# A two-layer decoder step: residual of the retention's output projection turned by VectorE's 32x32 transposes, with tiles of every second column

## The chip, the cores and the metric

The kernel runs on one core of a Trainium2 chip. The metric is the device time of one execution in microseconds (us); the time before is the median of three runs. The engines are TensorE (PE, with its weight loads as PEld), VectorE (DVE), ScalarE (ACT), GpSimd (POOL) and SyncE (SP). DMAs are issued by SP and by ACT; each of these issues in program order and waits in that order.

## The reference

One inference step of a trunk with two layers, for a prompt of 1024 tokens and for 8 single decode tokens (rows of x_sample). Layer one is multi-scale retention, layer two sliding-window attention; both are pre-normalized and residual. What matters here is the seam between them:

```python
    o = rmsnorm(o, g_out.reshape(RET_HEADS, RET_DV)).reshape(B, L, RET_V)
    o = o * jax.nn.silu(gate)
    return x + o @ w_out, S.astype(S0.dtype)
...
    h = rmsnorm(x, g_norm)
    proj = h @ w_in
```

D_MODEL is 1024, RET_V is 2048. So x + o @ w_out is a sum over 2048 features for 1024 output features and 1032 tokens, and its result, times a gain per feature, is the input of the attention's projection (w_in_swa, 1024 x 2304). All is float32.

## The kernel before

**Number format.** Every float32 operand of a large product is split into a high part (`hi`) and the rest (`lo`); a product is three matmuls (hi by hi, hi by lo, lo by hi) into one PSUM tile. The high part of a weight is made by ACT, the low part by DVE or POOL.

**Stages.** First the retention's input projection and the decode tokens' state update (up to about 540 us of the span), then the retention over chunks (`steps`, 32 of them, to about 690), then the output projection (`ro_` functions, about 683 to 878), then the attention layer (to the end). In the first two stages and in the block that holds `ro_ahead(2)` all engines run in program order; in the others PE does, and a planner orders ACT, DVE, POOL and SP.

**The output projection.** Activations are kept transposed (features on partitions, tokens along the row), so a result tile is 128 output features (`ft`, 8 of them) by a group of tokens (`gi`; `RG` is 0 to 512, 512 to 768, 768 to 1032). `ro_part` (L1197) adds 8 of the 16 blocks of 128 features in, three matmuls each; a tile has two parts (`kh`). The tiles of `gi` 0 come first, `ft` 0 to 7, then `gi` 1 and 2 for each `ft`. The weights come in slots of 1024 x 256 (`wslot`, L1137): two raws of 512 KB by SP, each converted in four pieces of 128x256, L1147 on ACT and L1148 on DVE, with the gain of the retention's output norm. Raws have two buffers (`wr`), slots three. `ro_ahead` (L1189) starts slots ahead of their use.

**The residual.** `ro_xr` (L1222) loads the x rows of a tile by SP (tile `xr`, two buffers; for `gi` 2 also 8 decode rows), and `ro_finish` (L1231) turns each 128x128 block on PE, through `tr` (L101), straight into the tile's PSUM sum:

```python
            for i in range(nfull):
                tr(ps[:, i * 128:i * 128 + 128], xr[:, i, :], ident, start=False, stop=(i == nfull - 1))
```

Then ACT copies the sum into `x1` (L1250), and for each 256 tokens ACT and DVE make the parts of the attention's input, `A_hi` and `A_lo`, from PSUM with the gain `gk` (L1252, L1253); ACT squares and POOL adds up for the norm; ACT stores `x1` to the scratch `xscr` (L1260). PSUM tiles come from two pools of 2 and 4. `reload2` (L1262) brings the first 512 tokens back from `xscr`, since `A_hi` holds the retention's output until then; the last projection of the attention layer (`so_all`, L1788) reads `xscr` once more as its residual.

**The early tile.** Tile (0, 0) is computed within the last two steps of the retention, in `b_wmm` (L1047). Its weights are loaded by `b_w` (L1026) in four loads of 512 rows by 128 columns and converted by `b_wc` (L1032) into `woh` and `wol`, its x rows by `b_x` (L1043). They stand in rings of tiles (`ring`, L163; `EV` at L161 gives the buffers: p 3, x 2, c 2, w 2), which the steps use for q and k (p), v (x) and the gate (c, w). A load into a ring waits until the tile that had the buffer is read: a q tile by b_ql on POOL (L812), a v tile by b_vl (L800). The loop over the steps is at L1078; `others` (L1059) is the order of a step's work on ACT, DVE and POOL; b_sq (L983, a square on ACT), b_ts (L991, DVE), b_pw (POOL, L116) and b_on (L999, DVE) normalize a chunk, and b_tr turns it on PE. A head's last state is stored by ACT's queue (L973, tile `sf`).

**Gains.** `small_loads` and `gains` turn three gain vectors into columns (`gcol`), early in the first stage.

Of the kernel before, what the change touches and what calls it, by code (L numbers as in the profile page):

```python
# [7 lines left out]
F32 = mybir.dt.float32  # L8
# [62 lines left out]
def _trunk(ctx, tc, nc, a):  # L71
# [17 lines left out]
    xscr = dp.tile([8, 128, NT], F32, name="xscr")  # L89
# [316 lines left out]
    gl = sp.tile([25, 128], F32, name="gl")  # L406
    rT = sp.tile([128, 7, 4, 4], F32, name="rT")
# [225 lines left out]
    later(15, lambda: act(gcol, heads[0].pop("pg")[:, :25], AF.Copy))  # L633
# [392 lines left out]
    def b_w(i):  # L1026

        t = ring("px"[i // 2])[:, 0:512].rearrange("p (k f) -> p k f", k=4)
        nc.sync.dma_start(out=t, in_=w_out_ret[i * 512:i * 512 + 512, 0:128].rearrange("(k p) f -> p k f", p=128))
        wo[i] = t  # L1030

    def b_wc(i):  # L1032

        raw = wo[i]
        hi, lo = [(woh[i + 2 * (x == "l")] if i < 2 else rp.tile([128, DV], F32R, tag="v" + x, name="wo" + x, bufs=2))
                  .rearrange("p (k f) -> p k f", k=4) for x in "hl"]
        for k in range(4):
            gk = gcol[:, 4 * i + k:4 * i + k + 1]
            act(hi[:, k], raw[:, k], AF.Copy, scale=gk)
            dve.scalar_tensor_tensor(lo[:, k], raw[:, k], gk, hi.bitcast(F32)[:, k], MUL, SUB)  # L1040
        wo[i] = hi, lo

    def b_x():  # L1043
        wo["x"] = ring("c")[:, 0:512].rearrange("p (c f) -> p c f", c=4)
        nc.sync.dma_start(out=wo["x"], in_=x_prompt[0, 0:512, 0:128].rearrange("(c p) f -> p c f", p=128))

    def b_wmm(i):  # L1047
# [3 lines left out]
        hi, lo = wo[i]  # L1051
# [26 lines left out]
    for i in range(-1, NS + 2):  # L1078
# [23 lines left out]
        for n in {NS - 2: (0,), NS - 1: (1, 2), NS: (3,)}.get(i, ()):  # L1102
            b_wc(n)
# [127 lines left out]
    def ro_finish(ft, gi):  # L1231
# [4 lines left out]
        if ft + gi:  # L1236
            if (ft, gi) not in ro_x:
                ro_xr(ft, gi)
# [765 lines left out]
```

## Time and profile before

| | us |
|---|---|
| three runs | 1313.51, 1311.6, 1314.25 |
| median | 1313.51 |
| profiled execution, its own time | 1314.25 |
| its span | 1312.2 |
| PE busy | 1284.0 (98%) |
| PEld busy | 1212.2 (92%) |
| DVE busy | 727.7 (55%) |
| ACT busy | 691.4 (53%) |
| POOL busy | 630.8 (48%) |

The profile is one execution on the chip. Matmuls overlap in their pipeline, so the busy time of a group of them is no measure of what one costs; the distance between the starts of neighbours is. "Idle before" stands in brackets, with what ended it. A line of a timeline joins neighbours of one kind (x4); its duration is that of all of them.

### The profile page before, as it was taken

The page shows a single profiled execution, that of the slowest core. Times are in us where ns is not written, and L with a number is a line of the kernel's source. Part 1 is how long each engine was busy: PE and PEld are TensorE (multiplying, and loading weights), DVE is VectorE, ACT ScalarE, POOL GpSimd, SP SyncE. Part 2 cuts the span into 40 slices and gives each one's busy share as a digit, 9 for nine tenths or more (in the row PEclk, how much of TensorE's full clock was granted, in tenths as well). Part 3 has the DMA queues.
Part 4 walks back from the last instruction along what each step waited for, and adds up shares of the span by engine and source line. Part 5 has one row for each costly group of instructions (what it writes and reads, how often), then busy time and mean ns, then how long its engine had stood idle before and what let it go on. Part 6 is the DMA issues. An engine that isn't in the chain of part 4 may idle for free.

```text
span 1312.2 us, 26102 instructions
## 1 busy us (share of the span) xinstructions
PE 1284.0 (98%) x9597; PEld 1212.2 (92%) x9597; DVE 727.7 (55%) x1476; ACT 691.4 (53%) x1722; POOL 630.8 (48%) x800
## 2 busy tenths in 40 slices
PE   6999999999999999999999999999999999999998
PEld 6999999999999999887887889999999999998998
DVE  6944556565565564477785333324665666766321
ACT  5533544554555653577775444445576666666121
POOL 6654544545445544599980110137476676554000
PEclk9999999999999999999999999999998999999999
DMA  6314767677676854456556554353032211237232
GB/s 225 104 61 129 238 197 244 180 234 220 197 239 184 247 174 138 132 169 213 177 165 193 162 165 123 122 147 85 17 106 72 65 58 44 75 110 251 73 96 78
DMA packets 199907, 193.98 MB, mean 148 GB/s; under 512 B 12916, under 2 KB 180140, under 8 KB 199764
## 3 DMA queue, kind: packets, MB, share of 16 engines
q1 hardware_dynamic: 165024, 157.78, 39.2%
q10 hardware_dynamic: 34756, 34.53, 8.3%
q8 instruction: 76, 1.25, 0.4%
q14 instruction: 51, 0.42, 0.1%
HBM read 132.23 MB, written 61.08 MB: 147 GB/s over the span
## 4 chain that ended last, share of the span: by engine, by line
PE 91%; DVE 2%; ACT 2%; DMA 2%; POOL 2%; issue 1%; ACTq 0%; SPq 0%; POOLq 0%; DVEq 0%
PE b L331 7%; PE b L332 7%; PE b L333 7%; PE pj L1167 6%; PE pj L1168 6%; PE pj L1169 6%; PE tr L101 4%; PE b L324 4%; PE b L325 4%; PE b L326 4%; PE pj L1214 4%; PE pj L1215 4%; PE pj L1216 4%; PE o L1645 2%; PE b L538 2%; PE sc L1610 1%
## 5 line engine op out<-in xcount | busy, mean ns | idle before, releaser
L331 PE MATMUL b<-xh,woh 128*128 128x258 f32 x784 | 223.2, 285 | 0.0
L333 PE MATMUL b<-xh,wol 128*128 128x258 f32 x784 | 221.7, 283 | 0.0
L332 PE MATMUL b<-xl,woh 128*128 128x258 f32 x784 | 221.6, 283 | 0.0
L1167 PE MATMUL pj<-A_hi,wh 128*128 128x384 f32 (+1 forms) x512 | 174.9, 342 | 1.7 <-ACT A_hi L1670 1.3
L1168 PE MATMUL pj<-A_lo,wh 128*128 128x384 f32 (+1 forms) x512 | 165.2, 323 | 0.1
L1169 PE MATMUL pj<-A_hi,wl 128*128 128x384 f32 (+1 forms) x512 | 165.1, 322 | 0.0
L331 PEld LDWEIGHTS b<-xh,woh 128*128 128x128 f32 x784 | 148.0, 189 | 4.1 <-issue 3.7
L332 PEld LDWEIGHTS b<-xl,woh 128*128 128x128 f32 x784 | 148.7, 190 | 0.0
L333 PEld LDWEIGHTS b<-xh,wol 128*128 128x128 f32 x784 | 148.0, 189 | 0.0
L222 POOL TENSOR_TENSOR wol<-raw,woh 128x512 fp32r<-128x512 f32 x52 | 68.1, 1318 | 130.9 <-ACT woh L217 128.8
L324 PE MATMUL b<-woh,xh 128*128 128x256 f32 x448 | 126.6, 283 | 0.0
L325 PE MATMUL b<-wol,xh 128*128 128x256 f32 x448 | 126.0, 281 | 0.0
L326 PE MATMUL b<-woh,xl 128*128 128x256 f32 x448 | 125.6, 280 | 0.0
L1167 PEld LDWEIGHTS pj<-A_hi,wh 128*128 128x128 f32 x512 | 97.3, 190 | 5.4 <-issue 2.6
L1168 PEld LDWEIGHTS pj<-A_lo,wh 128*128 128x128 f32 x512 | 97.5, 190 | 0.4 <-DVE A_lo L1671 0.4
L1169 PEld LDWEIGHTS pj<-A_hi,wl 128*128 128x128 f32 x512 | 96.9, 189 | 0.0
L1148 DVE SCALAR_TENSOR_TENSOR wl<-wr,gcol,wh 128x256 fp32r<-128x256 f32 x128 | 53.8, 486 | 68.2 <-ACT wh L1147 68.2
L1259 POOL TENSOR_TENSOR acc<-acc,sq 128x256 f32<-128x256 f32 (+1 forms) x28 | 20.6, 742 | 146.4 <-ACT sq L1258 146.3
L1625 POOL TENSOR_TENSOR s<-s,sm 128x512 f32<-128x512 f32 x64 | 66.5, 1039 | 47.7 <-DVE sm L1624 43.5
L324 PEld LDWEIGHTS b<-woh,xh 128*128 128x128 f32 x448 | 84.3, 188 | 5.0 <-issue 2.9
L326 PEld LDWEIGHTS b<-woh,xl 128*128 128x128 f32 x448 | 84.3, 188 | 0.0
L325 PEld LDWEIGHTS b<-wol,xh 128*128 128x128 f32 x448 | 84.3, 188 | 0.0
(391 smaller groups left out, 3636.6 us busy)
## 6 DMA issues: line engine op xcount, KB each, us to landing
raw<-in_w_in_ret_dram ACTq DMA_DIRECT2D x44, 512.0 KB
st<-in_state_ret_dram SPq DMA_DIRECT2D x64, 256.0 KB
out_dram<-st SPq DMA_DIRECT2D x64, 256.0 KB
wr<-in_w_out_ret_dram SPq DMA_DIRECT2D x32, 512.0 KB
wr<-in_w_in_swa_dram SPq DMA_DIRECT2D x18, 512.0 KB
vb<-vscr SPq DMA_DIRECT2D x64, 128.0 KB
evp<-qks SPq DMA_DIRECT2D x32, 256.0 KB
evx<-vsc SPq DMA_DIRECT2D x32, 256.0 KB
```

The lines of the kernel that those rows point to most:

```text
L222: eng.tensor_tensor(lo, src_of(s, name, sub), hi.bitcast(F32), SUB)
L324: mm(dst, xh, wh, start=a and i == 0, stop=False, skip_group_check=True)
L325: mm(dst, xh, wl, start=False, stop=False, skip_group_check=True)
L326: mm(dst, xl, wh, start=False, stop=z, skip_group_check=True)
L331: mm(dst, wh, xh, start=a, stop=False, **sg)
L332: mm(dst, wh, xl, start=False, stop=False, **sg)
L333: mm(dst, wl, xh, start=False, stop=z, **sg)
L1148: nc.vector.scalar_tensor_tensor(lo[:, k, :], raw[:, k % 4, :], gk, hi.bitcast(F32)[:, k, :], ALU.mult, ALU.subtract)
L1167: mm(ps, hi[:, k, fs], xh[:, k, t0:t1], start=first and k == ks[0], stop=False)
L1168: mm(ps, hi[:, k, fs], xl[:, k, t0:t1], start=False, stop=False)
L1169: mm(ps, lo[:, k, fs], xh[:, k, t0:t1], start=False, stop=last and k == ks[-1])
L1625: nc.gpsimd.tensor_tensor(st[:, :, 0:256], st[:, :, 0:256], sm.unsqueeze(2).broadcast_to([128, 2, 256]), ALU.mult)
```

## The change

A result tile no longer holds 128 neighbouring features but every second one of 256: feature 256 pr + 2 q + u stands at partition q of tile ft = 2 pr + u. So ACT and DVE read the weights of w_out_ret with a step of two columns, the gains of the attention's norm get columns in that order, and the rows of w_in_swa are loaded as pairs of rows per partition, in two transfers per raw (`rows_load`). The x rows are loaded for 256 tokens and 256 features at once, in four transfers of 32 partitions each, so that blocks of 32x32 already stand where they belong but for the turn within a block; DVE turns the blocks (`nc.vector.transpose`) and adds the PSUM sum. The scratch gets the shape [4, 128, 2, tokens]. The early tile's weights come in eight loads of 256 rows by 256 columns, of which half the columns are used; its residual (two loads) is still turned by PE.

```diff
-    xscr = dp.tile([8, 128, NT], F32, name="xscr")
+    xscr = dp.tile([4, 128, 2, NT], F32, name="xscr")
...
+        for u in range(2):
+            tr(pg[:, 32 + 4 * u:36 + 4 * u], gs.rearrange("a (p u) -> a u p", u=2)[:, u], ident[:4, :4])
...
+                        (gs, norm_swa.rearrange("o (a f) -> (o a) f", a=4)),
...
+        act(gcol[:, 16:24].rearrange("p (a u) -> p u a", u=2), pg[:, 32:40].rearrange("p (u a) -> p u a", u=2), AF.Copy)
...
+    def b_w(i, tag):
+
+        wo[i] = ring(tag)[:, 0:512].rearrange("p (k f) -> p k f", k=2)
+        nc.sync.dma_start(out=wo[i], in_=w_out_ret[i * 256:i * 256 + 256, 0:256].rearrange("(k p) f -> p k f", p=128))
+
+    def b_x(i, tag):
+
+        t = ring(tag)[:, 0:512].rearrange("p (c f) -> p c f", c=2)
+        nc.sync.dma_start(out=t, in_=x_prompt[0, 256 * i:256 * i + 256, 0:256].rearrange("(c p) f -> p c f", p=128))
+        wo["x", i] = t.rearrange("p c (q u) -> p c u q", u=2)[:, :, 0]
...
+        raw = wo[i].rearrange("p k (q u) -> p k u q", u=2)[:, :, 0]
...
+        for k in range(2):
+            gk = gcol[:, 2 * i + k:2 * i + k + 1]
+            act(hi[:, 2 * b + k], raw[:, k], AF.Copy, scale=gk)
+            dve.scalar_tensor_tensor(lo[:, 2 * b + k], raw[:, k], gk, hi.bitcast(F32)[:, 2 * b + k], MUL, SUB)
...
-        if i in (NS - 3, NS - 2):
-            b_w(i - NS + 3)
-        if i in (NS - 2, NS - 1):
-            b_w(i - NS + 4)
-        if i == NS - 1:
-            b_x()
+        for n, tag in {NS - 3: ((0, "p"),), NS - 2: ((1, "p"), (4, "x"), (2, "p")),
+                       NS - 1: ((5, "x"), (6, "c"), (3, "p"), (7, "p"))}.get(i, ()):
+            b_w(n, tag)
+        if i == NS:
+            b_x(0, "x")
+            b_x(1, "w")
...
-        for n in {NS - 2: (0,), NS - 1: (1, 2), NS: (3,)}.get(i, ()):
+        for n in {NS - 2: (0, 1), NS - 1: (2, 4, 3, 5), NS: (6, 7)}.get(i, ()):
...
+    def rows_load(raw, src, j):
+        for a in (0, 1):
+            r0 = 512 * j + 256 * a
+            nc.sync.dma_start(out=raw[:, 2 * a:2 * a + 2], in_=src[r0:r0 + 256].rearrange("(p u) f -> p u f", u=2))
...
+                h2, l2 = [t[:, k, :].rearrange("p (u q) -> p u q", u=2) for t in (hi, lo)]
+                r2 = raw[:, k % 4, :].rearrange("p (q u) -> p u q", u=2)
...
+                nc.scalar.activation(h2, r2, AF.Copy, scale=gk)
+                nc.vector.scalar_tensor_tensor(l2, r2, gk, h2.bitcast(F32), ALU.mult, ALU.subtract)
...
+    def ro_xd():
+        nc.gpsimd.memset(xd, 0.0)
+        v = x_sample[:, 0, :].rearrange("i (a b f) -> b i a f", a=4, b=4)
+        for b in range(4):
+            nc.sync.dma_start(out=xd[32 * b:32 * b + 8], in_=v[b])
+        for u in range(2):
+            nc.vector.transpose(xdT[:, :, u, :], xd.rearrange("p a (j u) -> p u a j", u=2)[:, u])
+
+    def ro_xr(pr, a):
+
+        xr = ro_x[pr, a] = fp.tile([128, 8, 64], F32, name="xr", bufs=4)
+        v = x_prompt[0, a:a + 256, 256 * pr:256 * pr + 256].rearrange("(a i) (b f) -> b i a f", i=32, b=4)
+        for b in range(4):
+            nc.sync.dma_start(out=xr[32 * b:32 * b + 32], in_=v[b])
...
-            if gi == 2:
-                tr(ps[:, 256:264], xr[0:8, 2, :], ident[:8, :8], start=False, stop=False)
-            for i in range(nfull):
-                tr(ps[:, i * 128:i * 128 + 128], xr[:, i, :], ident, start=False, stop=(i == nfull - 1))
...
-            pv = ps[:, a - t0:b - t0]
-            x1 = fp.tile([128, 264], F32, name="x1", bufs=2)
-            nc.scalar.activation(x1[:, :n], pv, AF.Copy)
+            x1 = fp.tile([128, 264], F32, name="x1", bufs=3)
+            if ft + gi == 0:
+                nc.vector.tensor_copy(x1[:, 0:256], ps[:, a - t0:a - t0 + 256])
+            else:
+                if (pr, a) not in ro_x:
+                    ro_xr(pr, a)
+                xr = ro_x[pr, a].rearrange("p a (j u) -> p u a j", u=2)
+                nc.vector.transpose(x1[:, 0:256], xr[:, u])
+                nc.vector.tensor_tensor(x1[:, 0:256], ps[:, a - t0:a - t0 + 256], x1[:, 0:256], ALU.add)
+            if n > 256:
+                nc.vector.tensor_tensor(x1[:, 256:264], ps[:, 256:264], xdT[:, pr, u, 0:8], ALU.add)
             if gi > 0:
-                nc.scalar.activation(A_hi[:, ft, a:b], pv, AF.Copy, scale=gk)
-                nc.vector.scalar_tensor_tensor(A_lo[:, ft, a:b], pv, gk, A_hif[:, ft, a:b], ALU.mult, ALU.subtract)
+                nc.scalar.activation(A_hi[:, ft, a:b], x1[:, :n], AF.Copy, scale=gk)
+                nc.vector.scalar_tensor_tensor(A_lo[:, ft, a:b], x1[:, :n], gk, A_hif[:, ft, a:b], ALU.mult, ALU.subtract)
...
-            nc.scalar.dma_start(out=xscr[ft, :, a:b], in_=x1[:, :n])
+            nc.scalar.dma_start(out=xscr[pr, :, u, a:b], in_=x1[:, :n])
...
         ro_finish(0, 0)
-        for ft in (1, 2):
-            ro_xr(ft, 0)
+        for a_ in (0, 256):
+            ro_xr(0, a_)
+        ro_xd()
```

## Rows read from the trace of the kernel before

**Rows 1.** The page's busy table, PE, and its chain by engine
```profile
PE 1284.0 (98%) x9597; PEld 1212.2 (92%) x9597; DVE 727.7 (55%) x1476; ACT 691.4 (53%) x1722; POOL 630.8 (48%) x800
...
PE 91%; DVE 2%; ACT 2%; DMA 2%; POOL 2%; issue 1%; ACTq 0%; SPq 0%; POOLq 0%; DVEq 0%
```

**Rows 2.** Instructions of L101 that read xr: count, ns min/median/max, first and last
```profile
L101 PE MATMUL pj<-ident,xr x68: 224/272/328, 707.6 to 877.8; 128*128 128x128 f32 x60, 8*128 8x8 f32 x8
```

**Rows 3.** Stretches: length, then busy us of PE, PEld, DVE, ACT, POOL, clock, DMA share, GB/s
```profile
705.00:710.00 5.00, 5.00 (x26) 4.07 (x25) 2.90 (x8) 3.87 (x10) 0.00 (x0) 1.00 0.86 257
...
820.00:840.00 20.00, 20.00 (x169) 19.84 (x168) 9.11 (x22) 10.92 (x27) 3.23 (x4) 1.00 0.43 129
```

**Rows 4.** Timeline of PE around three groups of transposes: start, duration, instruction
```profile
720.27 0.40 PE L1215 MATMUL pj<-A_lo,wh 128*128 128x512 f32 x1
720.50 0.39 PE L1216 MATMUL pj<-A_hi,wl 128*128 128x512 f32 x1
...
721.40 0.40 PE L1215 MATMUL pj<-A_lo,wh 128*128 128x512 f32 x1
...
784.71 0.28 PE L1216 MATMUL pj<-B_hi,wl 128*128 128x256 f32 x1
...
785.18 0.28 PE L1215 MATMUL pj<-B_lo,wh 128*128 128x264 f32 x1
...
790.73 0.28 PE L1216 MATMUL pj<-B_hi,wl 128*128 128x264 f32 x1
...
791.49 0.28 PE L1215 MATMUL pj<-B_lo,wh 128*128 128x256 f32 x1
```

**Rows 5.** Timeline of PE, its two waits after 710 us
```profile
714.66 0.51 PE L1216 MATMUL pj<-A_hi,wl 128*128 128x512 f32 x1 [0.23 <-DVE wl L1148]
...
717.78 0.51 PE L1214 MATMUL pj<-A_hi,wh 128*128 128x512 f32 x1 [0.52 <-ACT wh L1147]
```

**Rows 6.** Timeline of DVE: a cast in SBUF and an operation on PSUM, 128x256 each
```profile
671.43 0.28 DVE L806 CAST qh<-evp 128x256 fp32r<-128x256 f32 x1
...
672.82 0.48 DVE L775 SCALAR_TENSOR_TENSOR kl<-tr,M,kh 128x256 fp32r<-128x256 f32 x1
```

**Rows 7.** Timeline of SP's DMA issues, 675 to 710 us
```profile
675.78 0.38 SPq L1029 DMA_DIRECT2D evp<-in_w_out_ret_dram  x1
...
688.67 11.15 SPq L1144 DMA_DIRECT2D wr<-in_w_out_ret_dram  x4
699.98 0.94 SPq L1226 DMA_DIRECT2D xr<-in_x_prompt_dram  x2
703.64 6.25 SPq L1144 DMA_DIRECT2D wr<-in_w_out_ret_dram  x3
```

**Rows 8.** Timeline of POOL, the last read of a q tile
```profile
679.67 0.79 POOL L812 TENSOR_TENSOR ql<-evp,qh 128x256 fp32r<-128x256 f32 x1
```

**Rows 9.** Timeline of ACT and its DMA issues, 681 to 709 us
```profile
681.78 1.26 ACT L1039 ACTIVATE woh<-evp,gcol 128x128 fp32r<-128x128 f32 x4
...
684.12 0.57 ACT L987 ACTIVATE on<-po 128x512 f32<-128x512 f32 x1
...
685.78 0.38 ACTq L973 DMA_DIRECT2D out_dram<-sf  x1
...
695.59 3.31 ACT L1147 ACTIVATE wh<-wr,gcol 128x256 fp32r<-128x256 f32 x8 [4.61 <-PE S L101]
...
707.23 1.71 ACT L1147 ACTIVATE wh<-wr,gcol 128x256 fp32r<-128x256 f32 x4
```

**Rows 10.** Timeline of DVE, a chunk's scaling and the low parts of a raw
```profile
686.70 0.75 DVE L999 TENSOR_SCALAR on<-po,bss 128x512 f32<-128x512 f32 x1 [0.73 <-POOL bss L116]
...
710.75 1.69 DVE L1148 SCALAR_TENSOR_TENSOR wl<-wr,gcol,wh 128x256 fp32r<-128x256 f32 x4 [1.26 <-ACT wh L1147]
```

**Rows 11.** Timeline of PE, the last chunk's transposes
```profile
689.00 0.60 PE L101 MATMUL tr<-ident,on 128*128 128x128 f32 x4
```

**Rows 12.** Waits of SP's queue, 670 to 900 us: total, times, longest
```profile
SPq L1144 <- DMA out_dram<-sf: 9.7, 1, 9.7
```

More of the change, by code (lines that the diff above doesn't have):

```diff
@@ L406, in _trunk @@
     gl = sp.tile([25, 128], F32, name="gl")
+    gs = sp.tile([4, 256], F32, name="gs")
     rT = sp.tile([128, 7, 4, 4], F32, name="rT")
@@ L632, in _trunk, with gains_ev @@
     later(14, gains)
-    later(15, lambda: act(gcol, heads[0].pop("pg")[:, :25], AF.Copy))
+    def gains_ev():
+        pg = heads[0].pop("pg")
+        act(gcol, pg[:, :25], AF.Copy)
+        act(gcol[:, 16:24].rearrange("p (a u) -> p u a", u=2), pg[:, 32:40].rearrange("p (u a) -> p u a", u=2), AF.Copy)
+    later(15, gains_ev)
     later(17, lambda: [fn(T3, c) for c in (5, 7) for fn in (th, tl)])
@@ L1024, in _trunk @@
     wo = {}
[L1026 to L1030, printed above, removed]
-    def b_wc(i):
[L1034 to L1045, printed above, removed]
+    def b_w(i, tag):
[5 more added lines that the diff above has]
+        wo["x", i] = t.rearrange("p c (q u) -> p c u q", u=2)[:, :, 0]
+    def b_wc(i):
+        raw = wo[i].rearrange("p k (q u) -> p k u q", u=2)[:, :, 0]
+        n, b = i // 2, i % 2
+        if b == 0:
+            wo["c", n] = [(woh[n + 2 * (x == "l")] if n < 2 else rp.tile([128, DV], F32R, tag="v" + x, name="wo" + x, bufs=2))
+                          .rearrange("p (k f) -> p k f", k=4) for x in "hl"]
+        hi, lo = wo["c", n]
+        for k in range(2):
+            gk = gcol[:, 2 * i + k:2 * i + k + 1]
+            act(hi[:, 2 * b + k], raw[:, k], AF.Copy, scale=gk)
+            dve.scalar_tensor_tensor(lo[:, 2 * b + k], raw[:, k], gk, hi.bitcast(F32)[:, 2 * b + k], MUL, SUB)
     def b_wmm(i):
@@ L1126, in load @@
             raws[j] = wp.tile([128, 4, 256], F32, tag="wr", bufs=2, name="wr")
-            nc.sync.dma_start(out=raws[j], in_=v[:, 4 * j:4 * j + 4, :])
+            rows_load(raws[j], src, j)
         def conv(i):
@@ L1135, in wslot_parts, with wslot @@
         return (hi, lo), load, conv
[L1137 removed]
+    def wslot(src, gain=None, out=False, turn=True):
         hi = wp.tile([128, 8, 256], F32R, tag="wh", bufs=3, name="wh")
         lo = wp.tile([128, 8, 256], F32R, tag="wl", bufs=3, name="wl")
[L1141 removed]
         for j in range(2):
             raw = wp.tile([128, 4, 256], F32, tag="wr", bufs=2, name="wr")
[L1144 to L1145 removed]
+            if out or not turn:
+                nc.sync.dma_start(out=raw, in_=src[512 * j:512 * j + 512].rearrange("(k p) f -> p k f", p=128))
+            else:
+                rows_load(raw, src, j)
+            for k in range(4 * j, 4 * j + 4) if out else ():
+                h2, l2 = [t[:, k, :].rearrange("p (u q) -> p u q", u=2) for t in (hi, lo)]
+                r2 = raw[:, k % 4, :].rearrange("p (q u) -> p u q", u=2)
                 gk = gcol[:, gain + k:gain + k + 1]
[L1147 to L1149 removed]
+                nc.scalar.activation(h2, r2, AF.Copy, scale=gk)
+                nc.vector.scalar_tensor_tensor(l2, r2, gk, h2.bitcast(F32), ALU.mult, ALU.subtract)
             step = 2 if hi_act[0] else 4
[L1151 removed]
+            for i in range(0, 4, step) if not out else ():
                 js = slice(4 * j + i, 4 * j + i + step)
@@ L1215, in ro_part @@
             mm(ps, hi[:, k, fs], xl, start=False, stop=False)
-            mm(ps, lo[:, k, fs], xh, start=False, stop=False)
+            mm(ps, lo[:, k, fs], xh, start=False, stop=(not first and k == 7))
             yield 3 * n / 2400.0
```

38 lines of the change are left out of this document (10 added, 28 removed).

## The prediction

> **What bounds the kernel now.** I read the page's busy table and its chain first [rows 1]: TensorE (PE) is busy for 98% of the span and holds 91% of the chain that ended last, so a matmul taken out shortens the span unless PE then waits for something else. Next come the instructions that read the residual tile: 60 transposes of 128x128 and 8 of 8x8 on PE, all between 707 and 878 us [rows 2]. That is the retention's output projection. There a chunk of weights (512 KB, a "raw") is loaded by SP, turned into a high part on ScalarE (ACT) and a low part on VectorE (DVE), and used by PE. The stretches of that stage [rows 3] show two regimes. From 705 to 710 us the DMA engines are 86% busy: the weight supply is the limit. From 820 on PE never stops, DVE works 9 of 20 us and ACT 11. So a PE saving counts in full in the second regime, and in the first only as far as the weights keep up.
>
> **Transposes that leave PE.** They stand in 23 groups. Of a group I take the distance from the last matmul before it to the second one after it, less two ordinary matmul distances [rows 4]. For 512 columns: 720.50 to 721.40 is 0.90, less 2 x 0.235 (720.27 to 720.50 is 0.23), so 0.43; there are 7. For 256 columns: 784.71 to 785.18 is 0.47, less 2 x 0.115 (half the columns, half the distance), so 0.24; there are 8. For 264 columns with the small transpose: 790.73 to 791.49 is 0.76, less 0.24, so 0.52; there are 8. The sum is 3.0 + 1.9 + 4.2 = 9.1 us. The first group, at 707.6, saves nothing: PE next stands still at 714.66 and 717.78 for weights that come late [rows 5], and only earlier weights move that. So 8.6 us are to be had behind 718 us. The four transposes of the very first tile stay on PE.
>
> **What takes their place.** Per 256 columns DVE gets one transpose by 32x32 blocks and one addition out of PSUM. The addition goes by the 128x256 operation on PSUM at 0.48 [rows 6]. No such transpose is in the trace: the 128x256 cast, 0.28, bounds it below, twice the PSUM operation, 0.96, above; I take 0.35, near the cast, which also only moves 256 elements. Two of each per 512-column tile, or per pair of the small ones, is 1.7 us (2.9 at the upper end) in about 12 us. DVE, at 9.1 of 20 us [rows 3], goes to 12 (14). Hidden, since a finished tile sits in one of six PSUM buffers and the next tile takes 5.8 us or more; without that cover each of the 23 tiles would wait 0.8 to 1.4 us. ACT loses its copy. Two tiny transposes join at the gains, in a PE-bound place: 0.2 us (0 to 0.24, what two large ones cost). Weights loaded by two transfers instead of one in the attention stage, the reload from the re-shaped scratch and the extra small load I put at nothing: rows keep their length, and SP has long gaps there; without these each extra issue would cost 0.47.
>
> **The early tile's weights.** Here waits are added. Now SP issues the second of this tile's loads at 675.78 [rows 7] and the others as ring buffers come free. The new third load (rows 512 to 767, ring p) takes the buffer of the last q, which POOL reads until 679.67 + 0.79 = 680.46 [rows 8]. Four more loads stand behind it on SP, at 0.47 each, so the last leaves near 682.4. A raw of 512 KB was converted 3.6 us after its issue (703.64 [rows 7] to 707.23 [rows 9]); at 257 GB/s [rows 3] its bytes take 2.0, so 1.6 is fixed, and a load of 256 KB takes 1.0 more. The third load lands at 683.1, the fourth one behind, which is the other half of the second quarter, at 686.1. ACT, in program order, converts loads 2, 4, 3, 5 at 0.63 each and only then squares the last chunk, at 684.12 now [rows 9]; that slips to 687.4. The square (0.6), DVE's factor and POOL's power (0.73 of idle DVE) and DVE's scaling (0.75 [rows 10]) follow, so the last chunk's transposes on PE start near 690.0 instead of 689.00 [rows 11]: 1.0 us lost. Lower end 0, if the loads come 1 us sooner; upper end 3.3, ACT's whole slip. The same slip moves the state's store from 685.78 [rows 9] to 689.1. The first load of the projection waits for that store (9.7 us in SP's waits [rows 12]); it left at 688.67 and now leaves at 692.0, so it lands at 695.6. ACT can't use it before that anyway: PE holds its target until 695.6 [rows 9], and now until 696.6. No further cost.
>
> **The weight supply at the stage's start.** SP issued two x loads from 699.98 (0.94 for both, 0.47 each) and the fifth raw at 703.64, when its buffer came free [rows 7]. After the change SP issues eight x loads and four for the decode rows first: 12 x 0.47 = 5.6 us, until 705.6, or 706.6 with the 1.0 from above. The fifth raw is then converted 3.6 later, at 710.2, PE starts the second tile at 710.6 instead of 708.6, and waits once more for raw 7, whose buffer comes free only when raw 5 is converted (ACT 4 x 0.43 [rows 9], DVE 1.69 behind it [rows 10]). PE passes the point of 717.78 at about 719.8. That is 2.0 us, the 1.0 included. The next pair's eight x loads can fall between raws 6 and 8: up to 3.8 us of SP's time, of which I put 0.7 on the path, since SP mostly stands waiting for a buffer there. Ends: 0 and 3.8.
>
> **Sum.** 8.6 - 0.2 - 2.0 - 0.7 = 5.7 us less. The profiled execution took 1314.25 us (span 1312.2); it is the slowest of the three, 0.74 above their median of 1313.51. So the forecast for the median is **1307.8**. Reads of every second column in the conversions I cost at nothing; the upper end is rival C.
>
> The x loads now come in pieces of 256 B. The old ones, of 512 B, lie in the stretch with DMA at 0.86 [rows 3]; no row has 256 B in that volume. The Trainium skill (DMA: Bandwidth & Descriptors, section Specifications) wants at least 512 B per piece for line rate. If half the rate follows, the first pair's 512 KB hold the engines as 1 MB does, 4.1 us at 257 GB/s instead of 2.0, raw 5 is 2 us later, and the sum is 3.7 us less, 1309.8.
>
> **Rivals.**
> A. The supply is not delayed: SP's twelve issues fit into waits and the early tile's loads land in time. For it: SP waits for conversions through most of this stage. Against: the fifth raw left the moment it could. Then 9.1 - 0.2, and perhaps the 1.1 us of waits at 714 and 717 come back as well: 1303.5 to 1304.6.
> B. The supply eats nearly all: the second pair's eight loads stand ahead of raw 7 (3.8 in place of 0.7), and transfers in flight hold up the raws by 2 us more. For it: 86% DMA. Against: behind 720 us there is slack, since a raw comes every 2.9 us (two buffers, 3.6 + 0.5 + 1.7 a round) and two tiles of 11.6 us use four. Gain 5.7 - 5.1 = 0.6: 1312.9, no difference that can be measured.
> C. Slower: ACT and DVE read every second column, and such a read takes over twice as long. Place: the weight conversions, 0.43 each now. At 2.5 times, a raw's conversion takes 2.6 us longer; two buffers share that, so six raws come 6 x 1.3 = 7.8 late, the first piece 0.6, and the eight conversions ahead of the last square, 0.32 each, 3.8. That is -5.7 + 12.2 = +6.5: 1320. It decides from about 2.1 times. For it: no row reads that way, so it is open. Against: DVE's low part reads two operands in the time in which ACT reads one, so reading is not what limits either.
> The Trainium skill (SBUF — State Buffer, section Door 1) says that full rate needs two hits in each 16-byte line, which a step of two fp32 just gives; by that C falls. No row here shows it.
>
> **How the numbers follow.** A difference under 0.2% (2.6 us) can't be told from none. The forecast, 0.58, and A, 0.12, make faster 0.70; B, 0.18, makes the same; C and what I don't see, 0.12, slower. The range runs from A's better end, 1303, to just past B, 1313.5; it leaves out C and a little of the edges.
>
> **What would show it.** No reads of the residual tile by PE, and ordinary distances between tiles' matmuls. SP's third load of the early tile near 680.5, the last square near 687, a PE wait of about 1 us ahead of the last chunk's transposes. Twelve SP issues before the fifth raw, near 706.6, and PE waits of 2 to 3 us in all from there to 720. After that no PE wait, DVE near 12 of 20 us, and the stage's end some 6 us earlier. I am wrong if PE waits behind 725 us, if a conversion takes longer than 0.43, or if the gain is lost again in the attention stage.

## The result and the profile after

The changed kernel takes **1319.57 us** (five runs, 1315.6 to 1320.88) beside 1313.51 of the kernel before: ratio 1.0042 [1.0027, 1.0057], slower by some 6 us where 5.7 less were forecast, and outside the range (1303.0 to 1313.5). Its profiled execution took 1319.57, with a span of 1317.8, 5.6 more than the span of before. Three stretches, cut by TensorE's own instructions, say where:

| stretch of the profiled execution | before | after | difference |
|---|---|---|---|
| start to the last matmul of the retention's last chunk | 681.4 | 680.1 | -1.4 |
| from there to the early tile's last weights | 13.3 | 16.9 | +3.6 |
| the other tiles of the projection, to the first k/v matmul | 183.2 | 184.0 | +0.8 |
| attention and the rest, to the end of the span | 434.3 | 436.8 | +2.5 |

The first line is nothing of the change's: but for two tiny transposes at the gains that part is the same work, and over all profiles on record it takes 679.3 to 681.9. The table sums to 5.5.

The page's busy table, TensorE (PE) first, and the chain by engine, of the kernel after; they answer to [rows 1]:

```profile
PE 1276.4 (97%) x9531; PEld 1205.6 (91%) x9531; DVE 755.9 (57%) x1548; ACT 687.3 (52%) x1691; POOL 631.7 (48%) x801
...
PE 89%; POOL 2%; DVE 2%; DMA 2%; ACT 2%; issue 1%; SPq 0%; ACTq 0%; POOLq 0%; DVEq 0%
```

PE is busy 7.6 us less, with 66 matmul records fewer, and the span is longer: work left PE and idle time came. The waits of PE from 680 to 800 us (total, times, longest) show most of it:

```profile
PE pj L1233 <- ACT wh L1167: 8.7, 2, 8.1
PE tr L101 <- DVE on L1008: 3.1, 2, 1.9
PE S L1067 <- ACT woh L1056: 1.3, 1, 1.3
```

Before, the same stretch had these, and the 0.23 for low parts in [rows 5]:

```profile
PE tr L101 <- DVE on L999: 1.2, 1, 1.2
PE pj L1214 <- ACT wh L1147: 1.1, 2, 0.6
```

The new waits on PE's timeline:

```profile
687.68 0.51 PE L1067 MATMUL S<-A_hi,woh 128*128 128x512 f32 x1 [1.26 <-ACT woh L1056]
...
691.25 0.63 PE L101 MATMUL tr<-ident,on 128*128 128x128 f32 x4 [1.91 <-DVE on L1008]
...
718.31 0.79 PE L1233 MATMUL pj<-A_hi,wh 128*128 128x512 f32 x1 [8.06 <-ACT wh L1167]
...
720.18 0.63 PE L1234 MATMUL pj<-A_lo,wh 128*128 128x512 f32 x1
720.61 0.63 PE L1235 MATMUL pj<-A_hi,wl 128*128 128x512 f32 x1
```

The long one stands ahead of feature tile 2, the second tile behind the early one (feature tile 0); the prediction and the expectations call it the second tile. In the kernel before that tile starts without a wait, right behind the residual's transposes at 707.6; the 0.23 and 0.52 of [rows 5] lie inside it. Behind the long wait two matmuls are 0.43 apart (720.18 to 720.61) instead of 0.23 [rows 4], since the granted clock has fallen. Stretches of the same kernel (columns as in [rows 3]):

```profile
710.00:712.00 2.00, 0.24 (x2) 0.00 (x0) 1.04 (x3) 0.61 (x2) 0.72 (x1) 1.00 0.56 195
712.00:714.00 2.00, 0.00 (x0) 0.00 (x0) 0.26 (x1) 0.42 (x1) 0.72 (x1) 1.00 0.23 76
714.00:716.00 2.00, 0.00 (x0) 0.00 (x0) 0.32 (x2) 0.00 (x0) 0.00 (x0) 0.53 0.16 47
...
720.00:722.00 2.00, 2.00 (x6) 1.52 (x6) 1.76 (x5) 1.26 (x4) 0.00 (x0) 0.50 0.39 81
722.00:724.00 2.00, 2.00 (x6) 1.54 (x5) 0.00 (x0) 0.47 (x2) 0.00 (x0) 0.50 0.86 281
724.00:726.00 2.00, 2.00 (x9) 1.64 (x8) 1.73 (x4) 1.31 (x4) 0.00 (x0) 0.91 0.76 224
```

PE stood from 710, the clock went to 0.50 (the lower level, 1.2 GHz) near 714 and came back near 724.4. Some 14 matmuls, between 718.3 and 724.3, ran at a distance of 0.427 instead of 0.233: 14 x 0.194 = 2.7 us on top of the 8.06.

SP's issues tell why the weights were late; they answer to [rows 7]:

```profile
692.98 9.36 SPq L1160 DMA_DIRECT2D wr<-in_w_out_ret_dram  x4
702.44 5.47 SPq L1256 DMA_DIRECT2D xr<-in_x_prompt_dram  x8
711.19 3.00 SPq L1247 DMA_DIRECT2D xd<-in_x_sample_dram  x4
714.30 0.94 SPq L1160 DMA_DIRECT2D wr<-in_w_out_ret_dram  x2
```

The eight x loads ended at 707.9, 5.5 us after the first (3.8 of issues, and 1.7 of waiting for a raw ahead of them to land). Then SP stood 3.2 us ahead of the four loads for the decode rows, and the fifth raw left at 714.30, not near 706.6. SP's waits from 680 to 740 us name what it stood for:

```profile
SPq L1160 <- DMA out_dram<-sf: 8.0, 1, 8.0
...
SPq L1247 <- DMA xscr<-x: 3.2, 1, 3.2
...
SPq L1247 <- POOL acc L1286: 0.8, 1, 0.8
```

That is the early tile's store to scratch, issued from ScalarE's (ACT) queue. The decode rows' loads need nothing of it. In the program as built, the transfers of SP and ACT are counted on eight completion counters that are handed round among them, and before a transfer goes out its queue waits until the one before it on its counter has landed. The first decode load has the counter of the early tile's store, and the fifth raw that of feature tile 1's first store. ACT's timeline shows both stores, behind the conversion of the fourth raw and the squares:

```profile
706.57 1.76 ACT L1167 ACTIVATE wh<-wr,gcol 128x256 fp32r<-128x256 f32 x4 [1.10 <-DMA wr<-in_w_out_ret_dram]
...
709.38 0.35 ACTq L1287 DMA_DIRECT2D xscr<-x  x1
...
710.75 0.33 ACTq L1287 DMA_DIRECT2D xscr<-x  x1
...
717.74 3.52 ACT L1167 ACTIVATE wh<-wr,gcol 128x256 fp32r<-128x256 f32 x8 [5.03 <-DMA wr<-in_w_out_ret_dram]
```

The store leaves at 709.38, the decode loads at 711.19, 1.8 us later; their 3.0 us of issue end at 714.19, and the raw follows. Its conversion starts 3.4 us after its issue, as forecast (3.6).

The third stretch that lengthened is the attention stage. Two of PE's waits there, of the changed kernel, and the first of them in the kernel before, which has none of the second:

```profile
PE pm L1547 <- ACT sq L1526: 3.6, 1, 3.6
...
PE tr L101 <- DVE kkl L1442: 1.0, 1, 1.0
```
```profile
PE pm L1519 <- ACT sq L1498: 2.1, 1, 2.1
```

The wait for `kkl`, the lower half of k, comes at 920.4, 39 us into the stage. DVE makes `kkl` from ACT's `kkh`, which now stands behind a square of the query norm, and that square stands behind a conversion that waits for its load. ACT's timeline, after and before:

```profile
916.39 0.63 ACT L1173 ACTIVATE wh<-wr 128x512 fp32r<-128x512 f32 x1 [2.17 <-DMA wr<-in_w_in_swa_dram]
917.05 0.49 ACT L1526 ACTIVATE sq<-pj 128x384 f32<-128x384 f32 x1
```
```profile
911.90 0.49 ACT L1498 ACTIVATE sq<-pj 128x384 f32<-128x384 f32 x1 [0.72 <-PE pj L1169]
...
914.16 1.15 ACT L1154 ACTIVATE wh<-wr 128x512 fp32r<-128x512 f32 x2
```

Before, the same square came 34.0 us after the stage's first matmul, ahead of the conversion; now it comes 36.1 after it. The wait of 3.6 us is a later one, for the square at 996.85, 116 us into the stage, and stands behind another wait of ACT:

```profile
995.94 0.52 ACT L1692 ACTIVATE oh<-ot 128x384 fp32r<-128x384 f32 x1 [3.64 <-POOL ot L1685]
```

At this place PE waited 3.1 to 3.7 us in the twelve profiles in which the weights come in two loads per raw, 1.8 to 2.1 in three of the four with one load, and 3.0 in the fourth (y_nores below): it goes with the two loads, but not with them alone, and its cause stays open in part.

### The profile page after: what moved, and what is told of

Read it like the earlier page. It is cut to its first block, busy times and chain, and to the rows that moved or that the text cites. A ratio compares the mean times of both kernels' runs of the same rounds, so it can differ in the third digit from the quotient of the medians.

```text
span 1317.8 us, 26084 instructions
## 1 busy us (share of the span) xinstructions
PE 1276.4 (97%) x9531; PEld 1205.6 (91%) x9531; DVE 755.9 (57%) x1548; ACT 687.3 (52%) x1691; POOL 631.7 (48%) x801
## 4 chain that ended last, share of the span: by engine, by line
PE 89%; POOL 2%; DVE 2%; DMA 2%; ACT 2%; issue 1%; SPq 0%; ACTq 0%; POOLq 0%; DVEq 0%
PE b L331 7%; PE b L332 7%; PE b L333 7%; PE pj L1186 6%; PE pj L1187 5%; PE pj L1188 5%; PE pj L1233 4%; PE pj L1234 4%; PE pj L1235 4%; PE b L324 4%; PE b L325 4%; PE b L326 4%; PE tr L101 4%; PE o L1673 2%; PE b L539 2%
## 5 line engine op out<-in xcount | busy, mean ns | idle before, releaser
L1645 ACT ACTIVATE s<-s,mx 128x257 f32<-128x257 f32 x128 | 64.2, 505 | 35.6 <-DVE mx L1643 34.7
```

The lines of the kernel that those rows point to most:

```text
L1645: nc.scalar.activation(st[:, j, :], st[:, j, :], AF.Exp, bias=mx[:, j:j + 1], accum_out=sm[:, j:j + 1])
```

## The experiments

Executions of the kernel before lie up to 0.5% apart on one chip, and its medians on the chips used here lie between 1309.4 and 1313.5, so each ratio is to the kernel before on the same chip. Even these ratios move: three kernels with stops of 7.75 to 8.06, the change, x5 and x7, have 1.0042, 1.0060 and 1.0088. So the experiments are best set beside one another on one chip: x1, x2, x4, y_early, x5, y_split, y_nores and z1 ran on one, x6 and x7 on another, x8 and x9 on a third. The three columns on the right are of the profiled execution: the projection behind the early tile, PE's longest stop for the projection's weights behind feature tile 1 (mostly the one ahead of feature tile 2), and the attention stage.

| kernel | median us | ratio | projection | stop | attention |
|---|---|---|---|---|---|
| before | 1313.51 | | 183.2 | 0.52 | 434.3 |
| after | 1319.57 | 1.0042 [1.0027, 1.0057] | 184.0 | 8.06 | 436.8 |
| x1_xd_late | 1317.39 | 1.0047 [1.0034, 1.0061] | 180.5 | 5.44 | 436.2 |
| x2_early_order | 1317.26 | 1.0042 [1.0027, 1.0057] | 183.2 | 8.02 | 436.2 |
| x4_feed | 1309.76 | 0.9993 [0.9981, 1.0005] | 178.4 | 2.87 | 435.9 |
| y_early | 1315.26 | 1.0034 [1.0019, 1.0049] | 183.8 | 1.05 | 431.3 |
| x5_stores_behind | 1319.56 | 1.0060 [1.0041, 1.0078] | 183.6 | 7.96 | 436.9 |
| y_split | 1313.55 | 1.0017 [1.0006, 1.0028] | 182.7 | 0.6 | 435.8 |
| y_nores | 1305.82 | 0.9954 [0.9936, 0.9972] | 176.0 | 1.28 | 435.2 |
| **z1_hybrid** | **1305.22** | **0.9958 [0.9945, 0.9971]** | 176.3 | 0.75 | 433.8 |
| x7_stores_pool | 1320.47 | 1.0088 [1.0071, 1.0105] | 182.0 | 7.75 | 436.2 |
| x6_stores_pool_xd_late | 1318.3 | 1.0063 [1.0048, 1.0078] | 181.1 | 5.57 | 436.7 |
| x9_bufs4 | 1317.23 | 1.0033 [1.0020, 1.0046] | 180.3 | 5.05 | 436.6 |
| x8_pool_bufs4 | 1312.53 | 0.9993 [0.9978, 1.0007] | 178.7 | 2.19 | 435.3 |

The theory from the trace: the early tile's stores hold SP back, and so the fifth raw. The rival: the eight x loads and the decode loads are simply too much for SP and the DMA engines at that place.

**Decode loads later** (x1_xd_late): they go out after feature tile 5, into a buffer of the x ring.

```diff
         for a_ in (0, 256):
             ro_xr(0, a_)
-        ro_xd()
...
         ro_tile(ft, 0)
+        if ft == 5:
+            ro_xd()
```

> The changed kernel, with the four loads of the decode rows (tile xd) moved from the start of the projection to behind its fifth tile. Theory one (a wait in SP's queue): the 8.1 us in which PE stands ahead of its second tile come from these four loads, which wait for the store of the early tile and stand ahead of the fifth raw on SP. Then the fifth raw is issued near 708 instead of 714.3, PE waits 1 to 2 us there, its clock stays at the full level, and the time is 8 to 11 us below the changed kernel: 1309 to 1311. Theory two (volume): the x rows in pieces of 256 B keep the DMA engines busy and the raws late; then the fifth raw is still converted after 715, the wait stays above 6 us and the time is within 2 us of the changed kernel.

This decides nothing yet: the time is some 2 us below (x5, which behaves as the change, took 1319.56 on this chip), but with intervals of the ratios that overlap; the stop fell from 8.1 to 5.4 us only, between the 1 to 2 of theory one and the 6 of theory two, and the raw's conversion still came at 716.75, as by theory two. The x loads ended at 709.7, and SP stood again until 712.77: the fifth raw now has the counter of the early tile's store, which left at 710.97, 1.8 us earlier. The wait moved from the decode loads to the raw itself.

**Early tile's loads in another order** (x2_early_order):

```diff
-NS - 2: ((1, "p"), (4, "x"), (2, "p")),
-NS - 1: ((5, "x"), (6, "c"), (3, "p"), (7, "p"))
+NS - 2: ((1, "p"), (4, "x"), (6, "c"), (5, "x"), (2, "p"), (3, "p")),
+NS - 1: ((7, "p"),)
...
-NS - 1: (2, 4, 3, 5)
+NS - 1: (2, 3, 4, 5)
```

> The changed kernel with the early tile's eight loads in another order on SP: 0, 1, 4, 6, 5, 2, 3, 7 instead of 0, 1, 4, 2, 5, 6, 3, 7, converted as 2, 3, 4, 5. Nothing else moves. If the waits of PE at 687.7 (1.26 us) and 691.3 (1.91 us) come from load 3 standing behind 5 and 6 in one burst, both go but for half a us, and the time falls by 2 to 3 us, to about 1317, the wait of 8 us behind it staying. If the bytes of the eight loads as such are the cause (twice those of before), the order changes nothing and the time stays within 1 us of 1319.6.

The wait for the early weights is gone and the wait of the last chunk's transposes fell from 1.91 to 1.12 us, not to the half us that was expected; the time is the forecast 1317, and the long stop stayed. So the early tile's 3 us are its own, and the long stop has another cause.

**All of the feed** (x4_feed): both edits, and the first eight x loads behind the second raw instead of behind the fourth.

```diff
-        ro_ahead(2)
-        ro_finish(0, 0)
+        ro_ahead(1)
         for a_ in (0, 256):
             ro_xr(0, a_)
-        ro_xd()
+        ro_ahead(2)
+        ro_finish(0, 0)
```

> The changed kernel with the loads of the decode rows late, the early tile's loads in the new order, and the first eight loads of x rows issued behind the second raw instead of the fourth. Theory one: SP is never ahead of a free raw buffer with other work; PE's waits between 680 and 720 fall to 3 us or less, the clock stays at the full level, and the 8.6 us of the transposes show: 1304 to 1308, below the kernel before. Theory two: waits of over 6 us stay in that stretch, 1312 or more.

The fifth raw left at 704.02, and by the ratio the whole loss went: 9.8 us less than x5 on the same chip. Neither theory's figures came: PE's waits between 680 and 720 sum to 6.7 us, the clock fell to 0.50 again, and 1309.76 lies between the two ranges. A stop of 2.87 us stayed, on VectorE (DVE): one of its transposes waited 3.90 us for a store to scratch, ahead of the raw's low parts. ACT's issue of the store, and the transpose:

```profile
706.20 0.35 ACTq L1287 DMA_DIRECT2D xscr<-x  x1
```
```profile
710.60 0.45 DVE L1274 STREAM_TRANSPOSE x<-xr 128x256 f32<-128x256 f32 x1 [3.90 <-DMA xscr<-x]
```

That pointed to the buffers of the sum `x1`: three of them, two taken by the early tile until its stores have landed.

**The early tile's part alone** (y_early): the kernel before with the eight loads of 256 KB and the two x loads of the changed kernel, columns contiguous.

```diff
-in_=w_out_ret[i * 512:i * 512 + 512, 0:128]
+in_=w_out_ret[i * 256:i * 256 + 256, 0:256]
```

> The kernel before with the early tile's weights in eight loads of 256 rows by 256 columns (of which the first 128 columns are used), in the order and rings of the change, and its x rows in two loads; everything else as before, PE still turns the residual. If these loads by themselves cost what the changed kernel's trace shows, PE waits about 1.3 us in the second quarter and about 1.9 us ahead of the last chunk's transposes, and the time is 3 to 4 us above before: 1316.5 to 1317.5. If they are hidden, within 1 us of 1313.5.

3.9 us slower by the medians, 4.5 by the ratio, a little more than the 3.6 of the second line of the first table. That stretch itself takes 16.1 us here, 2.8 more than before: most of the line is this part's.

**Stores behind the loads** (x5_stores_behind):

```diff
-        ro_finish(0, 0)
         for a_ in (0, 256):
             ro_xr(0, a_)
-        ro_xd()
+        ro_xd_load()
+        ro_finish(0, 0)
+        ro_xd_turn()
```

> The changed kernel with one move in program order at the start of the projection: the eight x loads and the four sample loads are issued ahead of the early tile's two stores instead of behind them, and the early tile's evacuation follows them. The same transfers, the same bytes. Theory of the shared counter (a DMA waits until the one before it on its completion counter has landed; in the changed kernel the sample loads, in the run with the sample loads late the fifth raw, wait for the early tile's stores): nothing on SP waits for those stores any more, the fifth raw is issued some 3 to 5 us earlier, near 710 instead of 714.3, TensorE's stop ahead of the second tile falls from 8.1 us to 3.5 to 5, and the time by 3 to 5 us to some 1315. Rival, the volume on SP's queue and on the DMA engines sets it: the fifth raw stays near 714, the stop near 8 us, the time within 1 us.

A miss that decides nothing: in the program as built the stores have the same counters as before the edit, since counters go by planned time and not by the order of the text. SP waited 3.1 us for the store again.

**Split loads alone** (y_split), the kernel before:

```diff
-            nc.sync.dma_start(out=raws[j], in_=v[:, 4 * j:4 * j + 4, :])
+            for a in (0, 2):
+                nc.sync.dma_start(out=raws[j][:, a:a + 2], in_=v[:, 4 * j + a:4 * j + a + 2, :])
```

(The same in `wslot`, for the attention's weights.)

> The kernel before, with one part of the change alone: every raw of the attention's w_in_swa (and k/v) comes in two loads of 256 KB instead of one of 512 KB, rows in the old order. If the double number of loads, with the place that the planner then finds for the conversions, is what cost the attention stage 2.5 us (there TensorE waited 3.6 us instead of 2.1 for the square of the query norm and 1.0 us for the lower half of k): the attention stage is 2 to 3 us longer than before, the time 2 to 3 us over that of before, ratio near 1.002. If the stage's loss comes from the new row order, the new scratch layout or the new phase at which the stage starts: within 0.5 us of before.

Ratio 1.0017, some 2.2 us, as expected; of the stage's 2.5 us this profile has 1.5, short of the 2 to 3 expected. ACT's timeline has the order of the changed kernel, the square 35.8 us into the stage:

```profile
910.93 0.63 ACT L1157 ACTIVATE wh<-wr 128x512 fp32r<-128x512 f32 x1 [1.82 <-DMA wr<-in_w_in_swa_dram]
911.58 0.49 ACT L1501 ACTIVATE sq<-pj 128x384 f32<-128x384 f32 x1
```

**The term removed** (y_nores), the kernel before:

```diff
-            if gi == 2:
-                tr(ps[:, 256:264], xr[0:8, 2, :], ident[:8, :8], start=False, stop=False)
-            for i in range(nfull):
-                tr(ps[:, i * 128:i * 128 + 128], xr[:, i, :], ident, start=False, stop=(i == nfull - 1))
```

> The kernel before without TensorE's transposes of the residual in the 23 groups after the early tile; the loads of x stay, nothing adds x, so the output lacks the residual of all tiles but the early one. It measures the term removed. Forecast of the prediction's first term: 9.1 us, of which 8.6 usable: 1302 to 1303 beside 1311 to 1312 of before, ratio 0.993 to 0.9935. Rival, the transposes lay partly in time in which TensorE would wait anyway: 2 to 6 us.

The projection is 7.2 us shorter (183.2 to 176.0), the time by the ratio 6.0 (3.7 to 8.4). PE waits 2.6 us for weights instead of the 1.3 of before. The forecast (1302 to 1303, ratio up to 0.9935) was missed: 6.0 is the upper edge of the rival's 2 to 6. The 7.2 and the 1.3 of added waits make 8.5, close to the 8.6 that the prediction called usable; so the term's size is about right, but with the old feed 1.3 of it turns into waits. About 7.2 in the stage is what the change can bring with that feed.

**Costs avoided** (z1_hybrid): contiguous columns for feature tiles 0 and 1, with x in pieces of 128 B there; the early tile's four loads of before; the feed of x4_feed; four buffers for the sum.

```diff
-            x1 = fp.tile([128, 264], F32, name="x1", bufs=3)
+            x1 = fp.tile([128, 264], F32, name="x1", bufs=4)
...
+        if pr == 0:
+            v = x_prompt[0, a:a + 256, 128 * ft:128 * ft + 128].rearrange("(a i) (b f) -> b i a f", i=32, b=4)
```

> The changed kernel with its costs avoided: the first two feature tiles keep contiguous columns, so that the early tile has the four loads of the kernel before; x for the second tile is loaded behind the second raw, x of the samples after the sixth tile, and the tile that takes the sum has four buffers instead of three. VectorE's transposes serve all 23 groups. By the theory (removed 9.1; early tile at the waits of before; supply waits of 1 to 2 us left ahead of tiles 1 and 2; attention stage 2.5 us longer) 1311.4 - 9.1 + 1.5 + 2.5 = 1306, ratio 0.995 to 0.997. Rival, the gain is not on the path: within 0.2% of before.

1305.22 us, the fastest of all: by the ratio some 5.5 us less than the kernel before on its chip, and 14.3 less than x5, which has the change's stop, on the same chip (11 by the two kernels' ratios). PE's waits from 680 to 800 us in it:

```profile
PE pj L1230 <- ACT wh L1164: 2.4, 4, 1.3
PE tr L101 <- DVE on L1008: 1.2, 1, 1.2
PE pj L1232 <- DVE wl L1165: 0.8, 1, 0.8
```

The projection, 176.3, is as short as y_nores's 176.0, which has none of DVE's new work: in this stage that work costs PE next to nothing.

**The two links apart.** Four kernels: the decode loads late in each, and of the two suspects, the counter and the sum's buffers, none, one or both out of the way. First the stores of feature tiles 0 and 1 on GpSimd's queue, which has other counters, without (x7) and with (x6) the decode loads late.

```diff
-            nc.scalar.dma_start(out=xscr[pr, :, u, a:b], in_=x1[:, :n])
+            (nc.gpsimd if gi == 0 and ft < 2 else nc.scalar).dma_start(out=xscr[pr, :, u, a:b], in_=x1[:, :n])
```

> The changed kernel with one edit: the four stores to scratch of the early tile and of the second tile are issued from GpSimd's queue instead of ScalarE's. SP's issues, their order and their bytes stay as they were; only, no DMA of SP shares a completion counter with those stores any more. Counter theory (the sample loads waited for the early tile's store, the fifth raw for the second tile's first store): SP goes from the x loads straight to the sample loads and the fifth raw, which is issued near 711 instead of 714.3; TensorE's stop ahead of the second tile falls from 8.1 us to some 5, the time by 3 to 4 us to 1315.5 to 1316.5. Rival, volume (the DMA engines or SP's own issue time set the fifth raw): 714 or later, the stop near 8 us, the time within 1 us of 1319.6.

No gain, for a reason of the edit's own: SP now waited 4.2 us for the clearing of the decode rows on GpSimd, which stood behind the stores in that queue (`POOL xd L1244`, at 710.52).

> The same edit on top of the kernel whose sample loads come after the sixth tile (it had the fifth raw at 712.8, and a stop of 5.4 us). Counter theory: the fifth raw right behind the eight x loads, near 708 (707 to 709), the stop 1 to 2.5 us and no stretch at half clock behind it, time 1312 to 1314. Rival, volume: the fifth raw after 711, the stop over 4 us, the time within 1 us of 1317.4.

Half of it came true. The fifth raw left right behind the x loads, at 708.24, as the counter theory says and the rival does not, but its conversion did not follow, and the time is only 2.2 us below x7's. SP, DVE and ACT of this kernel:

```profile
703.93 4.21 SPq L1256 DMA_DIRECT2D xr<-in_x_prompt_dram  x8
708.24 2.29 SPq L1160 DMA_DIRECT2D wr<-in_w_out_ret_dram  x2
```
```profile
715.31 0.45 DVE L1274 STREAM_TRANSPOSE x<-xr 128x256 f32<-128x256 f32 x1 [3.29 <-DMA xscr<-x]
```
```profile
716.25 0.42 ACT L1285 ACTIVATE sq<-x 128x256 f32<-128x256 f32 x1 [3.78 <-DVE x L1275]
716.57 3.43 ACT L1167 ACTIVATE wh<-wr,gcol 128x256 fp32r<-128x256 f32 x8
```

The second link: DVE's fourth sum needs a buffer that the early tile's store still reads, ACT's square waits for DVE, and the conversion, whose raw has landed, stands behind the square on ACT. The store was issued from GpSimd at 711.03 and freed the buffer some 4 us later, where ACT's took 1.8 in x1; so here the edit made the second link worse. That is not the queue's doing: in x7, with the DMA engines at a share of 0.30, a store from GpSimd freed its buffer after some 2.2 us,

```profile
709.22 1.31 POOL L1287 DMA_DIRECT2D xscr<-x  x2 [12.93 <-DVE x L1269]
```
```profile
711.52 0.45 DVE L1274 STREAM_TRANSPOSE x<-xr 128x256 f32<-128x256 f32 x1 [0.78 <-DMA xscr<-x]
```

and in x4 one from ACT took 4.3, at a share of 0.94. In x6 the raws now left ahead of the store, and the share was 0.81 while it waited. Hence the last two kernels, with `bufs=4` on top of x1 and of x6.

> The kernel with late sample loads, and four buffers instead of three for the tile that takes the sum; the stores stay on ScalarE's queue. If the shared counter alone is enough to hold the fifth raw: it is issued near 712.8 again, and TensorE's stop ahead of the second tile stays at 4.5 to 5.5 us, time within 1.5 us of 1317.4. If the buffer wait was the only one that counted: the stop falls to 1 to 2 us and the time to 1312 to 1314.

> Late sample loads, the early and the second tile's stores from GpSimd's queue, and four buffers for the sum: neither the counter nor the buffer holds anything. If these two links are the cause, one behind the other: the fifth raw right behind the x loads as in the run before (708.2), its conversion some 4 us earlier than the 716.6 there, the stop 1 to 2.5 us, no stretch at half clock, time 1311 to 1314. Rival, the volume of the transfers holds the raw's landing: the conversion still waits for its transfer, the stop stays over 4 us and the time within 1.5 us of 1318.

PE's timeline at feature tile 2, first x9, then x8:

```profile
715.29 0.79 PE L1233 MATMUL pj<-A_hi,wh 128*128 128x512 f32 x1 [5.05 <-ACT wh L1167]
```
```profile
713.76 0.50 PE L1233 MATMUL pj<-A_hi,wh 128*128 128x512 f32 x1 [2.19 <-ACT wh L1167]
```

With the counter in place the stop is 5.4 and, with four buffers, 5.05 (its fifth raw left at 710.72, in a profile that ran 1.8 us earlier throughout); without the counter 5.6, and with both gone 2.2, and 4.7 us of the time are back (x9 to x8 on one chip, 1317.23 to 1312.53). The bytes were the same in all four, and in x8 the fifth raw's conversion, at 713.20, waits for no transfer: the rival, that volume holds the raw's landing, fell. Volume still acts through the store, whose landing it delays. One point of the expectation missed: the clock fell behind this stop too, to 0.53 and 0.62 in the two stretches of 2 us from 714 on.

**Both kernels again** (b0_again, a0_again: no edit), for the scatter of a single profile.

> The kernel before once more, for a second profile: how far two profiles of one program differ in the attention stage (434.3 us from its first k/v matmul to the end of the span). If the 2.5 us by which the changed kernel's attention stage is longer is the change's, this profile lies within 0.7 us of 434.3; if it is scatter of the stage, 1.5 us or more away.

> The changed kernel once more, for a second profile: the stop ahead of the second tile near 8 us and the half-clock stretch behind it again, if they are the program's and not one execution's. Attention stage within 0.7 us of 436.8 if its lengthening belongs to the change; 435.3 or less if it is scatter.

The stop is 7.89 in the second profile of the change, at 1321.49 us. The attention stage is 433.0, 1.3 from 434.3 and so between the marks that the expectation set, and 436.4. Over all profiles it is 431.3 to 435.2 where its weights come in one load each (four of them), 433.8 to 436.9 where they come in two (twelve): 2.6 longer on average, with up to 2.3 us of scatter on either side. Part of this scatter is the clock. Near 1258 us it stood at 0.50 for 3.4 us in most profiles, but not in b0_again, y_early, x8_pool_bufs4 and z1_hybrid; that costs 1.7 us. The kernel before in its two profiles (columns as in [rows 3]):

```profile
1256.00:1264.00 8.00, 8.00 (x46) 7.95 (x46) 1.20 (x4) 1.57 (x6) 0.00 (x0) 0.79 0.34 107
```
```profile
1256.00:1264.00 8.00, 8.00 (x59) 7.97 (x59) 1.20 (x4) 1.75 (x6) 0.00 (x0) 1.00 0.42 132
```

Less what half clock costs in each profile (there and near 992), the stage takes 429.2 to 430.1 with one load and 430.4 to 431.9 with two: without overlap, and 1.6 apart on average. So about 1.6 of the 2.6 is seen with the two loads, and z1_hybrid's 433.8 is short because it lacks the stretch at 1258 (430.4 without half clock, beside 430.7 in y_split).

## Why the prediction was wrong

**The step that failed** is "Twelve SP issues before the fifth raw, near 706.6": it gave each issue 0.47 us and no wait. The eight x loads were done at 707.91, where 0.47 each from 701.0 gives 704.8: 1.4 for a later start, 1.7 for a raw ahead of them that had to land. The larger part follows. SP is a queue, and the decode loads wait in it for the early tile's store, which is itself late: its sum stands on DVE behind the low parts of four raws, its square and store on ACT behind their high parts. SP stood 3.2 us for it, and the four decode loads took 3.0 instead of 1.9. Together that is 7.7 us on the raw (714.30 instead of 706.6), and 8.06 + 2.7 (clock) on PE, where the sum had 1.0 for the twelve issues, 2.0 with the early tile's 1.0. The text of the change shows no such dependence; SP's wait list of the first run does.

By stretches, the forecast was +1.0 for the early tile, -6.9 for the projection (-8.6 + 1.0 + 0.7), nothing for the attention stage, and +0.2 ahead of all three, at the gains. Measured are +3.6, +0.8 and +2.5, and ahead of them -1.4, which is not the change's. So 2.6, 7.7 and 2.5 were missing, and the failed step is the largest of them.

**Point by point.**
- Removed from PE, 9.1 with 8.6 usable: in the 23 groups no instruction of PE reads x's tile any more. The term's size about held; y_nores gives 7.2 in the stage, with 1.3 more of waits for weights, 8.5 in all.
- DVE's new work: a transpose takes 0.43 (0.35 forecast; below, its group of instructions: busy us, mean ns, idle before it), an addition 0.42 (0.48). DVE is busy 21.7 of 40 us from 820 on, 10.9 of 20 (12 forecast), and PE waits for nothing between 725 and the end of the stage. The sizes were off, the cover held.

```profile
L1274 DVE STREAM_TRANSPOSE x<-xr 128x256 f32<-128x256 f32 x30 | 12.7, 434 | 13.8 <-DMA xscr<-x 10.3 <-DMA xr<-in_x_prompt_dram 2.9 <-ACT sq L1285 0.6
```

- The early tile's weights, 1.0 (at most 3.3): 3.2 measured, at the upper end. The third load came about when forecast (converted at 682.28; forecast 683.1, less the 1.4 of the earlier start). The one behind it, for rows 768 to 1023, did not: its bytes were priced as if no more than the third's were in flight. Five loads of 256 KB went out between 679.1 and 682.5, and the DMA engines were full:

```profile
682.00:684.00 2.00, 2.00 (x12) 1.64 (x10) 1.25 (x4) 1.30 (x4) 0.00 (x0) 1.00 1.06 375
684.00:686.00 2.00, 2.00 (x10) 1.61 (x9) 0.00 (x0) 0.00 (x0) 0.00 (x0) 1.00 1.09 376
```

  Their 1.3 MB alone take 3.5 us at 375 GB/s. ACT stood 3.64 us for that load and converted it from 687.22, where the forecast (686.1, less the 1.4) is 684.7; the square came at 688.43, where the forecast of 687.4, less the 1.4, is 686.0.
- The attention stage, "at nothing": 2.5 us in the pair of profiles. y_split shows that the doubled loads alone cost about as much time (2.2 us by the ratio). They go with another order on ACT, which the planner chose and the prediction didn't look at; that order explains the wait of 1.0 us for `kkl`, while the rest of the loss is not traced to one cause. The prediction had named a loss in this stage as a way to be wrong.
- The second pair's x loads, 0.7: no wait behind 725, held.
- Rival C's time (1320) came true without its mechanism: ACT's four strided conversions take 1.76 to 1.77 us, where [rows 9] has 1.71, not 2.1 times as long. The Trainium skill (SBUF — State Buffer, section Door 1), by which C falls, agrees with that.
- Pieces of 256 B: from 708 to 709 they are alone, the x loads' own:

```profile
708.00:709.00 1.00, 1.00 (x6) 0.81 (x5) 1.00 (x4) 0.34 (x1) 0.00 (x0) 1.00 0.61 137
```

  That is 225 GB/s per full share (137 at 0.61), where the raw at 716 to 718 had 350 (378 at 1.08): about a third less. That pieces under 512 B fall short of the full rate agrees with the Trainium skill (DMA: Bandwidth & Descriptors, section Specifications); the half, the prediction's own guess beside it, is not borne out. By themselves the x loads put the raw off by the 3.1 us above, no more: in x6 it left right behind them.

## What to carry to other kernels

Before counting issues on a DMA queue, list for each new transfer what the queue will wait for at that point, the completion counters of other queues' transfers included: a small load that nobody needs yet can hold the weights behind a store. A new user of a ring of buffers needs the buffers for the transfers that still read them; here one more buffer decided whether moving the stores paid. And a saving on the bottleneck engine is worth having only with the feed that keeps it busy: with the same transposes on DVE the kernel is 5.5 us slower or 5.5 us faster than before, by how its loads, its stores and its first two tiles are laid out.

## What the runs showed of the hardware

- A stop can cost twice: in the changed kernel the granted clock was 0.50 from 714.1 to 724.3, 4 us of it within the stop of 8.06 and 6 behind it; with the stops of 2.19 and 2.87 us (x8, x4) it was 0.50 for 3.4 us. The stop's length alone doesn't say it: ahead of the last chunk, where the waits of the early tile are, the clock stayed at 1.00 in the changed kernel (waits of 1.26 and 1.91), and fell to 0.50 for 6.8 us in its second profile (waits of 1.9, 1.1 and 0.9); in the kernel before it fell near 1258 with no wait of PE over 0.7 us near.
- A store of 128 KB to scratch freed its buffer or its counter after 1.8 to 2.2 us where the DMA engines had a share of 0.30 to 0.43 (from ACT's queue in the change and x1, from GpSimd's in x7), and after some 4 us where it was 0.81 to 0.94 (from ACT's in x4, from GpSimd's in x6): the time went with the load on the engines and not with the queue.
- DVE's 32x32 transpose of 128x256 fp32 takes 0.43 us with every second column read, about as long as its addition out of PSUM (0.42).
